# First sublayer in a written order: adaLN weights in blocks of 256 features, two feature blocks modulated at a time

## Chip, cores and metric

One core of a Trainium2 chip runs the whole program once. The metric is the device time of that execution in microseconds (us); of several runs the median is taken.

## What is computed

Two transformer blocks with adaLN modulation over 256 tokens of `x` and 256 tokens of `ctx` (1024 features, float32), then a third hybrid layer and a final norm. The change touches the start of the first half-FFN of block 0:

```python
def adaln(cond, w, b):
    m = jax.nn.silu(cond) @ w + b
    return m.reshape(m.shape[:-1] + (N_MOD, D_MODEL))
def modulated_norm(h, g, m, k):
    return rmsnorm(h, g) * (1.0 + m[..., k + 1, :]) + m[..., k, :]
def swiglu(h, w_in, w_out):
    gate, up = jnp.split(h @ w_in, 2, axis=-1)
    return (jax.nn.silu(gate) * up) @ w_out
```

`h` is both the 256 rows of `x` and the 256 rows of `ctx`, each with its own condition vector. Before the first FFN product can be made, shift `m[0]` and scale `m[1]` (1024 features each, out of `ada_w`) have to be there.

## The kernel before

All work is in float32. A product is made of three matmuls (`mm3`, L142 to L144) of operands that are split into a high part (ACT copy, L132) and a low part (DVE subtraction, L133). The kernel is written in the Tile framework: pools give out buffers, and the framework's scheduler decides in which order the instructions stand on each engine, from the written order and its own model of time. Each engine then works through its own list strictly in that order.

Pools that matter: `rawp`, 5 buffers of 512 KB for loaded weights (`wdma`, L166); `wsp`, 8 buffers for split weights; the arena `ar`, 37 units of 512 KB; `psp`, 8 banks of PSUM.

`FirstFfn.start` (from L788) loads the four 128-row tiles of `x` and `ctx` (L797), scales each row by its root mean square (`stats`, steps to L533) and then goes through eight blocks `b` of 128 features:

- `dma_mod(b)`: two loads of 512 KB from `ada_w` (shift and scale), rows of 128 features, thus 512 B in one piece.
- `mod_products(b)`: 16 matmuls (L820) of the two condition vectors with these weights, then a copy by ACT (L823); `mod_columns(b)`: one small matmul (L828), and two DVE steps to `mods` and `amod` (L831, L832).
- `turn_in(b)`: four transposes (L838) of the scaled rows; `modulate(b)`: two ACT steps (L845), then the DVE cast to the high part (L848) and subtraction for the low part (L849) of `xT`.
- `products(b, q)`: for gate (`q` 0) and up (`q` 1) weights, two column blocks of three matmuls each over 512 tokens (L142 to L144).
- `dma_w(x)` and `split_w(x)`: the two halves (512 rows each) of the first 256 columns of gate and up weights.

After `start`, `setup_late` loads the bias of block 1 and three norm vectors by ACT's queue (L251, L243) and transposes them (L253). Then `body` makes the next pair of columns: `next_pair` loads two blocks for gate and two for up, splits them and goes on. PE's first matmul of that next pair is the mark used below for the end of the stage.

Far later in the program, `DiffAttention.setup` has a function `consts`; among its steps are a load of 128 single values, `subln`, by SP's queue (L945), and one DVE step that scales them (L946). They depend on nothing of the first sublayer.

Of the kernel before, what the change touches and what calls it, by code (L numbers as in the profile page):

```python
# [9 lines left out]
AF = mybir.ActivationFunctionType  # L10
ALU = mybir.AluOpType
AX = mybir.AxisListType

P = 128
D = 1024
KB = D // P
S = 256
# [73 lines left out]
class Kern:  # L91
# [48 lines left out]
    def mm3(self, out, lhi, llo, rhi, rlo, start, stop):  # L140
        mm = self.nc.tensor.matmul
        mm(out, lhi, rhi, start=start, stop=False)  # L142
        mm(out, lhi, rlo, start=False, stop=False)  # L143
        mm(out, llo, rhi, start=False, stop=stop)  # L144
# [60 lines left out]
    def setup(self):  # L205
# [29 lines left out]
        iv = self.ident.rearrange("p (h q r) -> p h q r", h=2, q=2)  # L235
        nc.vector.tensor_tensor(self.sel, iv[:, 0, :, 0:2], iv[:, 1, :, 0:2], ALU.add)

    def setup_late(self):
        nc, a, cp = self.nc, self.a, self.cp
        self.adab.append(self.cols(a["ada_b"][1].rearrange("(k p) -> k p", p=P), 72, "adab1"))  # L240
        n2 = self.scr([24, P])
        for i, nme in enumerate(("norm_ffn1_2", "norm_mix_2", "norm_ffn2_2")):
            nc.scalar.dma_start(n2[8 * i:8 * i + 8, :], a[nme].rearrange("b (k p) -> (b k) p", p=P))  # L243
        self.n2 = self.cols(None, 24, "n2c", rows=n2)

    def cols(self, src, n, name, rows=None):

# [537 lines left out]
class FirstFfn(ModFfn):  # L785


    def start(self):  # L788
        nc, k, a = self.nc, self.k, self.a
        self.begun = self.T  # L790
        self.xT = k.asplit(KB, self.T)
        self.xn = [None] * 4
        self.p = [[k.ps() for _ in range(2)] for _ in range(2)]
        self.w = [[None, None], [None, None]]
        self.h = [k.unit([P, D]) for _ in range(4)]
        for t in range(4):
            nc.sync.dma_start(self.h[t], (a["x"] if t < 2 else a["ctx"])[0, (t % 2) * P:(t % 2 + 1) * P, :])  # L797

        mod = []
        w = [None, None]  # L800

        def dma_mod(b):
            mod.append([
                k.wdma(a["ada_w"][0, :, q * D + b * P:q * D + (b + 1) * P].rearrange("(k p) c -> p k c", p=P),
                       [P, KB, P]) for q in range(2)])

        def dma_w(x):
            w[x] = [k.wdma(src[512 * x:512 * x + 512, c0:c0 + 256].rearrange("(k p) c -> p k c", p=P), [P, 4, 256])
                    for src, c0 in (self.wg, self.wu)]

        def split_w(x):
            for q in range(2):
                self.w[q][x] = k.wsplit(w[x][q])

        def mod_products(b):
            pm = k.ps()
            for kk in range(KB):
                for q in range(2):
                    g = 32 * (2 * (kk % 2) + q)
                    nc.tensor.matmul(pm[g:g + 32, 0:P], k.sc[:, kk, :], mod[b][q][:, kk, :],  # L820
                                     start=kk < 2, stop=kk >= KB - 2)
            ms = k.scr([P, P])
            nc.scalar.activation(ms, pm[:, 0:P], AF.Copy)  # L823
            return pm, ms

        def mod_columns(b, pm, ms):
            pc = pm[:, 256:260].rearrange("p (q s) -> p q s", q=2)
            nc.tensor.matmul(pc, ms, k.sel, start=True, stop=True)  # L828
            mv = k.mods[0].rearrange("p (m k) s -> p m k s", k=KB)[:, 0:2, b, :]
            bv = k.adab[0].rearrange("p (m k) -> p m k", k=KB)[:, 0:2, b:b + 1]  # L830
            nc.vector.tensor_tensor(mv, pc, bv.to_broadcast([P, 2, 2]), ALU.add)  # L831
            nc.vector.scalar_tensor_tensor(k.amod[0][:, 0, :, b], k.mods[0][:, KB + b, :], 1.0,  # L832
                                           k.ng[:, b:b + 1].to_broadcast([P, 2]), ALU.add, ALU.mult)

        def turn_in(b):
            pt = k.ps()
            for t in range(4):
                nc.tensor.transpose(pt[:, t * P:(t + 1) * P], self.xn[t][:, b * P:(b + 1) * P], k.ident)  # L838
            return pt

        def modulate(b, pt):
            f = k.scr([P, self.T])
            for s in range(2):
                sl = slice(s * S, (s + 1) * S)
                nc.scalar.activation(f[:, sl], pt[:, sl], AF.Identity,  # L845
                                     scale=self.scale(s)[:, b:b + 1], bias=self.bias(s)[:, b:b + 1])
            hi, lo = self.xT.at(0, b), self.xT.at(1, b)
            nc.vector.tensor_copy(hi, f)  # L848
            nc.vector.tensor_tensor(lo, f, hi.bitcast(F32), ALU.subtract)  # L849

        def products(b, q):
            for c in range(2):
                hi, lo = self.w[q][b // 4]
                cc = slice(c * P, (c + 1) * P)
                k.mm3(self.p[q][c], hi[:, b % 4, cc], lo[:, b % 4, cc], self.xT.at(0, b), self.xT.at(1, b),
                      b == 0, b == KB - 1)

        dma_mod(0)
        dma_w(0)
        for b in range(1, 4):  # L860
            dma_mod(b)
        o = Order()
        for t in range(4):
            steps, took = self.stats(t)
            o.steps(1.46 * t, steps)
        o.issue()
        pt = None
        for b in range(KB + 1):
            if b < KB:
                pm, ms = mod_products(b)  # L870
                nt = turn_in(b)
            if b == 0:
                split_w(0)
            if b:
                products(b - 1, 0)
            if b < KB:
                mod_columns(b, pm, ms)
                modulate(b, nt)
            if b == 2:
                dma_w(1)  # L880
            if b == 4:
                split_w(1)
            if 2 <= b < 6:
                dma_mod(b + 2)
            if b:
                products(b - 1, 1)


class PlainFfn(Ffn, Phase):
# [835 lines left out]
```

## Time and profile before

| what | us |
|---|---|
| median of 3 runs (2332.54 to 2335.16) | 2334.33 |
| the profiled execution, its own time | 2337.68 |
| its span, first to last instruction | 2335.8 |
| first matmul of the next pair (end of the stage) | 59.76 |

Over the span PE is busy 97%, DVE 65%, ACT 46%, POOL 4%. In a timeline each row gives start, duration, engine, line, operation, output and input tiles, and in brackets the idle time ahead of it with what ended it. In a table of windows each row gives, for a stretch, the busy time of each engine with its number of instructions, the granted clock of TensorE, the mean busy share of the 16 DMA engines and the rate of the loads in GB/s.

### The profile page before, as it was taken

How to read it: one execution, taken by the hardware profiler on the slowest of the kernel's cores; microseconds unless marked ns; L12 is line 12 of the kernel's file. 1: busy time of each engine (PE TensorE's matmuls, PEld its weight loads, DVE VectorE, ACT ScalarE, POOL GpSimd, SP SyncE). 2: the span in 40 equal slices, each digit the busy share in tenths (PEclk: the TensorE clock that was granted, in tenths of full speed). 3: DMA queues.
4: the chain of work that ended last, by engine and by line, in shares of the span. 5: the costliest groups of instructions: out<-in, count | busy, mean ns of one | idle time of the engine just before them, and what ended most of it. 6: DMA issues, size and time to landing. Idle time of an engine off the chain costs nothing.

```text
span 2335.8 us, 31186 instructions
## 1 busy us (share of the span) xinstructions
PE 2269.2 (97%) x11835; PEld 1910.5 (82%) x11835; DVE 1523.0 (65%) x2478; ACT 1063.1 (46%) x1975; POOL 84.4 (4%) x130
## 2 busy tenths in 40 slices
PE   7999999998899999999999999999999999999998
PEld 5888888877688788888888887788889887898887
DVE  4876474678767753746866626676666757887664
ACT  4322223566653222134323225666556647765553
POOL 0000000111110000000000001100000002000000
PEclk9999999999999999999999999999999999999999
DMA  9665374321225543652665442145665675545664
GB/s 283 206 190 180 108 235 135 100 64 46 82 73 162 180 145 105 214 168 73 199 186 170 163 148 71 63 152 177 195 198 173 188 243 145 149 122 190 179 183 143
DMA packets 270943, 361.31 MB, mean 155 GB/s; under 512 B 11472, under 2 KB 222280, under 8 KB 270792
## 3 DMA queue, kind: packets, MB, share of 16 engines
q1 hardware_dynamic: 270464, 359.17, 49.6%
q8 instruction: 93, 1.52, 0.3%
q14 instruction: 58, 0.48, 0.1%
q10 hardware_dynamic: 328, 0.14, 0.0%
HBM read 355.02 MB, written 4.24 MB: 154 GB/s over the span
## 4 chain that ended last, share of the span: by engine, by line
PE 60%; DVE 5%; ACT 2%; POOL 1%; issue 1%; DMA 1%; POOLq 0%; DVEq 0%; ACTq 0%
PE ps L142 14%; PE ps L143 14%; PE ps L144 14%; PE ps L151 9%; PE ps L153 5%; PE ps L154 1%; DVE wl L133 1%; DVE u L133 1%; ACT junk L371 1%; DVE u L409 1%; POOL sm L377 0%; DVE s_l L556 0%; ACT wh L132 0%; PE ps L545 0%; PE ps L288 0%
## 5 line engine op out<-in xcount | busy, mean ns | idle before, releaser
L133 DVE TENSOR_TENSOR wl<-raw,wh 128x1024 fp32r<-128x1024 f32 x458 | 550.6, 1211 | 369.6 <-ACT wh L132 347.0
L132 ACT ACTIVATE wh<-raw 128x1024 fp32r<-128x1024 f32 x458 | 475.1, 1047 | 527.1 <-PE ps L143 443.7
L142 PE MATMUL ps<-s_h,wh 128*128 128x512 f32 (+1 forms) x1312 | 491.5, 376 | 6.9 <-ACT u L1063 5.0
L143 PE MATMUL ps<-s_l,wh 128*128 128x512 f32 (+1 forms) x1312 | 489.8, 373 | 0.6
L144 PE MATMUL ps<-s_h,wl 128*128 128x512 f32 (+1 forms) x1312 | 488.5, 372 | 0.0
L275 DVE SCALAR_TENSOR_TENSOR u<-raw,sc,u 128x1024 f32<-128x1024 f32 x224 | 276.9, 1279 | 81.1 <-DMA raw<-in_ada_w_dram 81.0
L142 PE MATMUL ps<-wh,s_h 128*128 128x512 f32 x784 | 308.0, 393 | 0.0
L143 PE MATMUL ps<-wl,s_h 128*128 128x512 f32 x784 | 306.1, 390 | 0.0
L144 PE MATMUL ps<-wh,s_l 128*128 128x512 f32 x784 | 305.7, 390 | 0.0
L142 PEld LDWEIGHTS ps<-s_h,wh 128*128 128x128 f32 x1312 | 247.6, 189 | 56.8 <-ACT u L1063 6.2
L143 PEld LDWEIGHTS ps<-s_l,wh 128*128 128x128 f32 x1312 | 247.4, 189 | 44.5 <-DVE s_l L556 2.3
L144 PEld LDWEIGHTS ps<-s_h,wl 128*128 128x128 f32 x1312 | 247.5, 189 | 42.5
L151 PE MATMUL ps<-s_p,wh 128*128 128x512 f32 x1008 | 258.1, 395 | 1.4 <-DVE scr L160 1.4
L151 PEld LDWEIGHTS ps<-s_p,wh 128*128 128x128 f32 x1008 | 188.1, 189 | 37.6 <-DVE scr L160 1.3
L132 ACT ACTIVATE s_h<-scr 128x256 fp32r<-128x256 f32 (+1 forms) x144 | 73.3, 510 | 247.4 <-DVE scr L724 230.5
L144 PEld LDWEIGHTS ps<-wh,s_l 128*128 128x128 f32 x784 | 147.6, 188 | 31.0
L142 PEld LDWEIGHTS ps<-wh,s_h 128*128 128x128 f32 x784 | 147.8, 189 | 30.4 <-DVE scr L1115 0.2
L143 PEld LDWEIGHTS ps<-wl,s_h 128*128 128x128 f32 x784 | 147.7, 188 | 29.9
L153 PEld LDWEIGHTS ps<-s_p,wl 128*128 128x128 f32 x1152 | 157.9, 191 | 11.5
L153 PE MATMUL ps<-s_p,wl 128*128 128x256 f32 x1152 | 161.3, 283 | 0.0
L143 PE MATMUL ps<-u,s_h 128*128 128x512 f32 x264 | 103.9, 393 | 1.3 <-DVE u L133 1.3
L142 PE MATMUL ps<-u,s_h 128*128 128x512 f32 x264 | 104.2, 395 | 0.0
(209 smaller groups left out, 2735.0 us busy)
## 6 DMA issues: line engine op xcount, KB each, us to landing
raw<-in_ffn_w_in_dram SPq DMA_DIRECT2D x176, 512.0 KB, 4.3
raw<-in_ada_w_dram SPq DMA_DIRECT2D x144, 512.0 KB, 4.5
raw<-in_ffn_w_out_dram SPq DMA_DIRECT2D x88, 512.0 KB, 4.3
raw<-in_ffn_gate_dram SPq DMA_DIRECT2D x44, 512.0 KB, 4.8
raw<-in_ffn_up_dram SPq DMA_DIRECT2D x44, 512.0 KB, 4.7
raw<-in_ffn_down_dram SPq DMA_DIRECT2D x44, 512.0 KB, 4.4
raw<-in_w_in_dram SPq DMA_DIRECT2D x44, 512.0 KB, 4.3
raw<-in_da_w_in_dram SPq DMA_DIRECT2D x24, 512.0 KB, 3.8
```

The costliest lines, as they stand in the source:

```text
L132: self.nc.scalar.activation(hi, src, AF.Copy)
L133: self.nc.vector.tensor_tensor(lo, src, hi.bitcast(F32), ALU.subtract)
L142: mm(out, lhi, rhi, start=start, stop=False)
L143: mm(out, lhi, rlo, start=False, stop=False)
L144: mm(out, llo, rhi, start=False, stop=stop)
L151: mm(out, w(b)[0], x.both(b), start=b == 0, stop=False)
L153: mm(out[:, 0:S], w(b)[1], x.at(0, b), start=False, stop=False)
L154: mm(out, w(n - 1)[0], x.both(n - 1), start=False, stop=True)
L275: nc.vector.scalar_tensor_tensor(acc[s][h], raw, x, acc[s][h], ALU.mult, ALU.add)
L371: self.nc.scalar.activation(self.junk, src, AF.Square, scale=1.0 / 32, accum_out=ss)
L409: nc.vector.scalar_tensor_tensor(h[:, sl], st.yg[k], st.r, h[:, sl], ALU.mult, ALU.add)
```

## The change

- `ada_w` comes in pieces for two feature blocks: per pair `bp` four loads of 512 KB (rows of 256 features, 1 KB in one piece; 512 of the 1024 input rows each), straight into arena units and no longer into `rawp`.
- One pair's `mod_products` has 16 matmuls over 256 columns; `mod_columns` makes both blocks. So two blocks are modulated at a time.
- The units of the scaled rows are given out first (`o.issue()` stands before `dma_mod(1)`).
- Order by hand: the whole stage stands inside `with k.tc.manual_schedule()`; loads are issued up front, products of block `b` stand beside the preparation of later blocks.
- `setup_late`'s loads move to SP's queue at the end of the stage's loads (`load_late`), into an arena unit.

```diff
+    def load_late(self):
+        nc, a = self.nc, self.a
+        rows = self.unit([P, 2, P])
+        self.late_rows = rows[0:72, 0, :], rows[0:24, 1, :]
+        nc.sync.dma_start(self.late_rows[0], a["ada_b"][1].rearrange("(k p) -> k p", p=P))
+        for i, nme in enumerate(("norm_ffn1_2", "norm_mix_2", "norm_ffn2_2")):
+            nc.sync.dma_start(rows[8 * i:8 * i + 8, 1, :], a[nme].rearrange("b (k p) -> (b k) p", p=P))
...
-        def dma_mod(b):
-            mod.append([
-                k.wdma(a["ada_w"][0, :, q * D + b * P:q * D + (b + 1) * P].rearrange("(k p) c -> p k c", p=P),
-                       [P, KB, P]) for q in range(2)])
+        def dma_mod(bp):
+
+            mod.append([[k.unit([P, 4, S]) for _ in range(2)] for _ in range(2)])
+            for x in range(2):
+                for q in range(2):
+                    c0 = q * D + bp * S
+                    nc.sync.dma_start(mod[bp][q][x], a["ada_w"][0, 512 * x:512 * x + 512, c0:c0 + S]
+                                      .rearrange("(k p) c -> p k c", p=P))
...
-        dma_mod(0)
-        dma_w(0)
-        for b in range(1, 4):
-            dma_mod(b)
         o = Order()
         for t in range(4):
             steps, took = self.stats(t)
             o.steps(1.46 * t, steps)
-        o.issue()
-        pt = None
-        for b in range(KB + 1):
...
+        with k.tc.manual_schedule():
+
+            dma_w(0, 0)
+            dma_mod(0)
+            dma_w(1, 0)
+            o.issue()
+            dma_mod(1)
+            dma_mod(2)
+            for q in range(2):
+                dma_w(q, 1)
+            dma_mod(3)
+            k.load_late()
+            NP = KB // 2
+            turned = {0: turn_in(0)}
+            split_w(0, 0)
+            pm = mod_products(0)
+            turned[1] = turn_in(1)
+            mod_columns(0, *pm)
+            modulate(0, turned.pop(0))
+            split_w(1, 0)
+            modulate(1, turned.pop(1))
+            for bp in range(NP):
+                b = 2 * bp
+                last = bp == NP - 1
+                products(b, 0)
+                if bp == 0:
+                    products(b, 1)
+                if not last:
+                    pm = mod_products(bp + 1)
+                    turned[b + 2] = turn_in(b + 2)
+                if bp:
+                    products(b, 1)
+                if not last:
+                    mod_columns(bp + 1, *pm)
+                    modulate(b + 2, turned.pop(b + 2))
+                products(b + 1, 0)
+                if not last:
+                    turned[b + 3] = turn_in(b + 3)
+                    modulate(b + 3, turned.pop(b + 3))
+                if bp == 1:
+                    for q in range(2):
+                        split_w(q, 1)
+                products(b + 1, 1)
```

Where this puts instructions is seen in the order of the built programs. Names in brackets are the semaphores that an instruction waits for: `DMAHW0` to `DMAHW7` are eight counters that the loads are given in turn, so that a load first waits for the one that had its counter before.

DVE, before, near the end of the stage (`s_h_121` is the high part of blocks 6 and 7, `wl` the low parts of the next pair's weights):

```order
L133 TENSOR_TENSOR wl_608<-raw_603,wh_607 128x1024 [waits DMAHW5_49,Activation_49]
L848 CAST s_h_121<-scr_516 128x512 [waits Activation_49]
L849 TENSOR_TENSOR s_l_122<-scr_516,s_h_121 128x512 [waits DVE_49]
L133 TENSOR_TENSOR wl_612<-raw_605,wh_611 128x1024 [waits DMAHW6_49,Activation_49]
L946 TENSOR_SCALAR subln<-subln 128x1 [waits DMAHW0_49]
L831 TENSOR_TENSOR mods_103<-ps_527,adab_95 128x2x2 [waits PE_49]
L832 SCALAR_TENSOR_TENSOR amod_105<-mods_103,ng 128x2 [waits DVE_49]
```

DVE, changed, near its beginning (`s_h_115` is the high part of blocks 0 and 1, `s_h_117` that of blocks 2 and 3):

```order
L133 TENSOR_TENSOR wl_267<-raw_147,wh_266 128x1024 [waits DMAHW6_49,Activation_49]
L860 CAST s_h_115<-scr_270 128x512 [waits Activation_49]
L861 TENSOR_TENSOR s_l_116<-scr_270,s_h_115 128x512 [waits DVE_49]
L843 TENSOR_TENSOR mods_103<-ps_287,adab_95 128x2x2 [waits PE_49,Activation_49]
L844 SCALAR_TENSOR_TENSOR amod_105<-mods_103,ng 128x2 [waits DVE_49]
L843 TENSOR_TENSOR mods_103<-ps_287,adab_95 128x2x2
L844 SCALAR_TENSOR_TENSOR amod_105<-mods_103,ng 128x2 [waits DVE_49]
L976 TENSOR_SCALAR subln<-subln 128x1 [waits DMAHW4_49]
L860 CAST s_h_117<-scr_317 128x512 [waits Activation_49]
L861 TENSOR_TENSOR s_l_118<-scr_317,s_h_117 128x512 [waits DVE_49]
```

The step on `subln` stood behind the splits of the next pair's first weights and ahead of block 7; it now stands ahead of the high part of block 2.

SP's queue, before, near the end of the stage (`raw_603` and `raw_605` are the next pair's gate weights, `raw_627` and `raw_629` its up weights):

```order
L166 DMA raw_475<-in_ada_w_dram 128x8x128 [waits DMAHW7_49,PE_49]
L166 DMA raw_603<-in_ffn_w_in_dram 128x4x256 [waits DMAHW0_49,PE_49]
L166 DMA raw_605<-in_ffn_w_in_dram 128x4x256 [waits DMAHW1_49,PE_49]
L166 DMA raw_627<-in_ffn_w_in_dram 128x4x256 [waits DMAHW2_49,PE_49]
L945 DMA subln<-in_da_subln_dram 128x1
L166 DMA raw_629<-in_ffn_w_in_dram 128x4x256 [waits DMAHW5_49,DVE_49]
```

SP's queue, changed, from the last pair's four pieces on (`u_209` to `u_212`):

```order
L813 DMA u_209<-in_ada_w_dram 128x4x256 [waits DMAHW1_49]
L813 DMA u_211<-in_ada_w_dram 128x4x256 [waits DMAHW2_49]
L813 DMA u_210<-in_ada_w_dram 128x4x256 [waits DMAHW3_49]
L813 DMA u_212<-in_ada_w_dram 128x4x256 [waits DMAHW4_49]
L242 DMA u_217<-in_ada_b_dram 72x128 [waits DMAHW5_49]
...
L166 DMA raw_529<-in_ffn_w_in_dram 128x4x256 [waits DMAHW1_49]
L166 DMA raw_531<-in_ffn_w_in_dram 128x4x256 [waits DMAHW2_49,DVE_49]
L166 DMA raw_553<-in_ffn_w_in_dram 128x4x256 [waits DMAHW3_49,DVE_49]
L975 DMA subln<-in_da_subln_dram 128x1 [waits DMAHW4_49]
```

The load of `subln` stands in the same company as before, behind the next pair's blocks. Before, it waited for no counter; now it has the one that `u_212`, the last piece of `ada_w`, had before it.

ACT, changed, behind the two modulations of blocks 4 and 5 (`raw_205` and `raw_207` are the second halves of the first gate and up weights, `raw_529` and `raw_531` the next pair's gate weights):

```order
L857 ACTIVATE scr_402<-ps_397,mods_103,amod_105 128x256 [waits DVE_49,PE_49,Activation_49]
L857 ACTIVATE scr_402<-ps_397,mods_103,amod_105 128x256
L132 ACTIVATE wh_407<-raw_205 128x1024 [waits DMAHW7_49]
L132 ACTIVATE wh_411<-raw_207 128x1024 [waits DMAHW0_49]
L132 ACTIVATE wh_533<-raw_529 128x1024 [waits DMAHW1_49]
L132 ACTIVATE wh_537<-raw_531 128x1024 [waits DMAHW2_49,PE_49]
L832 ACTIVATE scr_444<-ps_427 128x256 [waits PE_49,Activation_49]
```

Before, the same splits stood ahead of the modulation of block 3 (lines L132 between L823 and L845):

```order
L132 ACTIVATE wh_417<-raw_317 128x1024 [waits DMAHW3_49]
L823 ACTIVATE scr_348<-ps_331 128x128 [waits PE_49,Activation_49]
L132 ACTIVATE wh_421<-raw_319 128x1024 [waits DMAHW4_49]
L845 ACTIVATE scr_364<-ps_350,mods_103,amod_105 128x256 [waits DVE_49,PE_49,Activation_49]
L845 ACTIVATE scr_364<-ps_350,mods_103,amod_105 128x256
```

They now follow the modulation of block 5, and block 4 is the first that uses them. From about the 270th row of PE on, the order on all engines is the same as before.

## Rows read from the trace of the kernel before

**Rows 1.** Windows of 10 us: busy time of each engine, granted clock, DMA share, GB/s.
```profile
20.00:30.00 10.00, 10.00 (x96) 7.40 (x94) 2.05 (x7) 2.45 (x6) 0.00 (x0) 1.00 1.12 298
50.00:60.00 10.00, 7.87 (x38) 5.43 (x34) 5.73 (x12) 5.12 (x9) 0.00 (x0) 1.00 0.66 230
60.00:70.00 10.00, 10.00 (x45) 8.26 (x45) 7.60 (x11) 3.24 (x4) 0.00 (x0) 1.00 0.57 190
```
**Rows 2.** Timeline of PE: first modulation, first product, one steady block, the stage's end.
```profile
14.51 1.93 PE L820 MATMUL ps<-raw,sc 128*32 128x128 f32 x30
...
19.93 1.63 PE L142 MATMUL ps<-s_h,wh 128*128 128x512 f32 x3
...
25.46 1.08 PE L820 MATMUL ps<-raw,sc 128*32 128x128 f32 x32
26.47 0.66 PE L838 MATMUL ps<-ident,u 128*128 128x128 f32 x4
26.89 0.47 PE L142 MATMUL ps<-s_h,wh 128*128 128x512 f32 x1
...
28.36 0.28 PE L828 MATMUL ps<-sel,scr 128*128 128x4 f32 x2
28.49 0.47 PE L142 MATMUL ps<-s_h,wh 128*128 128x512 f32 x1
...
30.06 1.08 PE L820 MATMUL ps<-raw,sc 128*32 128x128 f32 x32
...
59.12 0.25 PE L253 MATMUL ps<-ident,scr 72*128 72x72 f32 x1 [0.82 <-DMA scr<-in_ada_b_dram]
59.76 0.50 PE L142 MATMUL ps<-s_h,wh 128*128 128x512 f32 x1
```
**Rows 3.** Windows, for the rate of the loads (last column, GB/s).
```profile
0.00:9.00 9.00, 0.73 (x3) 0.46 (x3) 1.50 (x11) 3.99 (x9) 0.76 (x5) 1.00 0.73 256
9.00:12.00 3.00, 0.00 (x0) 0.00 (x0) 1.67 (x7) 2.87 (x9) 1.11 (x2) 1.00 1.18 303
53.00:57.00 4.00, 3.42 (x16) 2.52 (x15) 1.50 (x5) 1.02 (x2) 0.00 (x0) 1.00 1.04 388
7.00:8.00 1.00, 0.00 (x0) 0.00 (x0) 0.11 (x1) 0.94 (x5) 0.00 (x0) 1.00 1.01 410
```
**Rows 4.** Timeline of SP's queue: issue of a small load at the start, and of `subln`.
```profile
0.74 0.38 SPq L208 DMA_DIRECT2D ident<-in_k_ident_dram  x1
...
41.47 5.03 SPq L166 DMA_DIRECT2D raw<-in_ffn_w_in_dram  x3
46.54 0.50 SPq L945 DMA_DIRECT2D subln<-in_da_subln_dram  x1
```
**Rows 5.** Timeline of DVE: the step that waits for `ident`, and the stage's end.
```profile
2.93 0.16 DVE L236 TENSOR_TENSOR sel<-ident 128x4 f32<-128x4 f32 x1 [1.56 <-DMA ident<-in_k_ident_dram]
...
50.70 0.42 DVE L848 CAST s_h<-scr 128x512 fp32r<-128x512 f32 x1
51.16 0.69 DVE L849 TENSOR_TENSOR s_l<-scr,s_h 128x512 fp32r<-128x512 f32 x1
51.77 1.22 DVE L133 TENSOR_TENSOR wl<-raw,wh 128x1024 fp32r<-128x1024 f32 x1
53.22 0.15 DVE L946 TENSOR_SCALAR subln<-subln 128x1 f32<-128x1 f32 x1 [0.23 <-DMA subln<-in_da_subln_dram]
```
**Rows 6.** Timeline of ACT: one block's modulation and one split.
```profile
29.13 1.02 ACT L845 ACTIVATE scr<-ps,mods,amod 128x256 f32<-128x256 f32 x2 [2.22 <-DVE amod L832]
30.18 1.06 ACT L132 ACTIVATE wh<-raw 128x1024 fp32r<-128x1024 f32 x1
```
**Rows 7.** A long idle of PE far behind the stage, and the granted clock around it.
```profile
1976.13 0.69 PE L1431 MATMUL ps<-ident,u 128*128 128x128 f32 x2 [4.04 <-DVE u L1421]
...
1976.00:1981.00 5.00, 4.87 (x16) 4.20 (x17) 3.78 (x13) 2.22 (x8) 0.00 (x0) 0.50 0.36 105
1981.00:1982.00 1.00, 1.00 (x7) 0.92 (x6) 0.00 (x0) 0.05 (x1) 0.00 (x0) 0.62 0.00 0
```

More of the change, by code (lines that the diff above doesn't have):

```diff
@@ L236, in setup @@
         nc.vector.tensor_tensor(self.sel, iv[:, 0, :, 0:2], iv[:, 1, :, 0:2], ALU.add)
-    def setup_late(self):
[L239 to L244, printed above, removed]
+    def load_late(self):
[5 more added lines that the diff above has]
+            nc.sync.dma_start(rows[8 * i:8 * i + 8, 1, :], a[nme].rearrange("b (k p) -> (b k) p", p=P))
+    def setup_late(self):
+        self.adab.append(self.cols(None, 72, "adab1", rows=self.late_rows[0]))
+        self.n2 = self.cols(None, 24, "n2c", rows=self.late_rows[1])
+        del self.late_rows
     def cols(self, src, n, name, rows=None):
@@ L799, in start, with dma_w, split_w, mod_products @@
         mod = []
-        w = [None, None]
-        def dma_mod(b):
-            mod.append([
-                k.wdma(a["ada_w"][0, :, q * D + b * P:q * D + (b + 1) * P].rearrange("(k p) c -> p k c", p=P),
-                       [P, KB, P]) for q in range(2)])
[L807 to L815, printed above, removed]
+        w = {}
+        def dma_mod(bp):
[5 more added lines that the diff above has]
+                                      .rearrange("(k p) c -> p k c", p=P))
+        def dma_w(q, x):
+            src, c0 = (self.wg, self.wu)[q]
+            w[q, x] = k.wdma(src[512 * x:512 * x + 512, c0:c0 + 256].rearrange("(k p) c -> p k c", p=P), [P, 4, 256])
+        def split_w(q, x):
+            self.w[q][x] = k.wsplit(w[q, x])
+        def mod_products(bp):
             pm = k.ps()
@@ L819, in mod_products, with mod_columns @@
                     g = 32 * (2 * (kk % 2) + q)
-                    nc.tensor.matmul(pm[g:g + 32, 0:P], k.sc[:, kk, :], mod[b][q][:, kk, :],
+                    nc.tensor.matmul(pm[g:g + 32, 0:S], k.sc[:, kk, :], mod[bp][q][kk // 4][:, kk % 4, :],
                                      start=kk < 2, stop=kk >= KB - 2)
-            ms = k.scr([P, P])
-            nc.scalar.activation(ms, pm[:, 0:P], AF.Copy)
+            mod[bp] = None
+            ms = k.scr([P, S])
+            nc.scalar.activation(ms, pm[:, 0:S], AF.Copy)
             return pm, ms
[L826 to L833, printed above, removed]
+        def mod_columns(bp, pm, ms):
+            pc = pm[:, S:S + 8].rearrange("p (b q s) -> p b q s", b=2, q=2)
+            for x in range(2):
+                nc.tensor.matmul(pc[:, x], ms[:, x * P:(x + 1) * P], k.sel, start=True, stop=True)
+            for x in range(2):
+                b = 2 * bp + x
+                mv = k.mods[0].rearrange("p (m k) s -> p m k s", k=KB)[:, 0:2, b, :]
+                bv = k.adab[0].rearrange("p (m k) -> p m k", k=KB)[:, 0:2, b:b + 1]
+                nc.vector.tensor_tensor(mv, pc[:, x], bv.to_broadcast([P, 2, 2]), ALU.add)
+                nc.vector.scalar_tensor_tensor(k.amod[0][:, 0, :, b], k.mods[0][:, KB + b, :], 1.0,
+                                               k.ng[:, b:b + 1].to_broadcast([P, 2]), ALU.add, ALU.mult)
         def turn_in(b):
@@ L865, in start @@
             o.steps(1.46 * t, steps)
-        o.issue()
-        pt = None
-        for b in range(KB + 1):
[L869 to L886, printed above, removed]
+        with k.tc.manual_schedule():
[40 more added lines that the diff above has]
+                products(b + 1, 1)
 class PlainFfn(Ffn, Phase):
```

## The prediction

> **What bounds the kernel now.** I read the table of windows first. From 20 us on PE has no gap for thirty microseconds; between 50 and 60 us it is busy 7.87 of 10, and from 60 us on it is full again [rows 1]. Loads run at 298 GB/s beside it with the DMA engines marked as saturated (share 1.12) [rows 1]. So two resources are close to their limit in the stage, PE and the loads, and what the change can win lies in the gaps at its two ends.
>
> The timeline of PE gives the rhythm [rows 2]. A steady block starts with its modulation at 25.46 us and the next with its own at 30.06: 4.60 us. Of that the modulation's matmuls take 1.01 (25.46 to 26.47), the transposes 0.42 (to 26.89), the column matmul 0.13 (28.36 to 28.49), and the twelve products the rest, 3.04, so 1.52 for one half block. The first product starts at 19.93, the next pair's first matmul, which I take as the end of the stage, at 59.76; just ahead of it PE waits 0.82 us for a late load [rows 2]. From there on the order of all engines is unchanged and PE is full, so the difference at this mark passes on to the end.
>
> **What the change does, part by part.**
>
> *The step on `subln` in DVE's list decides.* In the order of the changed program DVE meets `subln` right behind the second pair of `mods`/`amod`, and the cast of block 2 is queued behind it. DVE takes its steps in that order. PE needs this cast for `products(2, 0)`, and everything PE has behind that, the modulation of blocks 4 and 5 included, stands behind it in PE's list. Before, the same step stood near the end of the stage and cost 0.23 us of DVE's time [rows 5].
>
> When does `subln` land? SP issues its load only when the counter it takes over has been released, that is when `u_212`, the last piece of `ada_w` for the stage, has landed. Up to there the stage has loaded 2.10 MB of `x` and `ctx`, 20 pieces of 512 KB (16 of `ada_w`, 4 of gate and up weights; 10.49 MB) and 0.16 MB of constants, 12.75 MB. By 9.0 us 256 GB/s have brought 2.30 MB [rows 3], and that part is unchanged in kind. For the other 10.45 MB the rate is open: 303 GB/s is what a stretch with much 512 B traffic shows, 388 one with rows of 1 KB and 4 KB, 410 one with 4 KB rows alone [rows 3]. The new pieces all have rows of 1 KB, so 388 is nearest: 26.9 us, landing at **35.9 us** (34.5 at 410, 43.5 at 303).
>
> Then the load itself. Before, SP issued it at 46.54 behind three blocks of weights issued from 41.47 on [rows 4], and DVE could go on at 53.22 [rows 5]: 6.7 us. Now it again stands behind three blocks of the next pair. The other end is a small load with nothing ahead of it, `ident`: issued at 0.74 [rows 4], used at 2.93 [rows 5], 2.2 us. I take 6.7, since the company is the same: DVE is released at **42.6 us** (38.1 by the other end). With 0.15 for the step, 0.42 for the cast [rows 5] and about 0.1 for the signal, PE goes on at 43.2.
>
> *What is left for PE from there*, all on the path: blocks 2 to 7 have 12 half blocks of 1.52, 18.2 us; two modulations (pairs 2 and 3); transposes of blocks 4 to 7, 4 times 0.42, 1.7; four column matmuls of 0.13, 0.5 [rows 2]. A modulation now has the same 16 matmuls over 256 columns in place of 128: between 1.01, if a matmul's cost is fixed, and 2.02, if it goes by columns; I take 2.02, as the columns are what streams, so 4.0. Together 24.5.
>
> *The clock.* While DVE waits, PE idles: blocks 0 and 1 are done by about 31 to 35 us, so for 8 us or more. Far behind, PE waits 4.04 us and then runs at a granted clock of 0.50, the 1.2 GHz level, from 1976.13 until about a quarter before 1982 [rows 7]: 5.6 us at half rate, 2.8 us lost. I add 2.8; the ends are 0 and, if it stays low twice as long, 5.6.
>
> *The splits of the second halves.* ACT now has them behind the modulation of block 5, and block 4's products are the first to need them. From the end of block 5's transposes: 1.02 us for its modulation and 1.06 for the split [rows 6], so the high part is there after 2.1, while PE has only one half block of 1.52 ahead: 0.6 us of wait. DVE has the cast, 0.42, the low part, 0.69, then the weights' low part, 1.22 [rows 5], ready after 3.4 to 3.5, which PE's third matmul wants at about 2.6: 0.8 to 0.9. Together **1.5 us** (0 if the half clock keeps PE behind).
>
> *Edits with no cost or gain here.* The first load order, the wider first modulation and the new order of blocks 0 and 1 all lie ahead of PE's wait and are covered by it; without that cover they are the first rival. The late loads now land long before they are wanted, which takes the 0.82 us away [rows 2]; the two transposes keep about 0.4. Raw buffers are no longer held by `ada_w`, so the next pair's weights are split inside the stage; the second pair of splits was so before.
>
> *Sum.* 43.2 + 24.5 + 2.8 + 1.5 + 0.4 = 72.4 us against 59.76: **12.6 us more**. The profiled execution takes 2337.68 us in all around a span of 2335.8, 3.35 above the median of the runs; it would become 2350.3, and the median of 2334.33 becomes **2346.9 us**, 0.54% more. About 0.2%, 4.7 us, can be told from no change.
>
> **A rule against this sum.** The row of mixed 512 B traffic gives 303 GB/s, the row with longer pieces 388 [rows 3]; I read that as a gain of the longer pieces. The Trainium skill ("DMA: Bandwidth & Descriptors", Specifications) says that transfers reach line rate from 512 B on, which would leave the loads as slow as they are. The two rows speak against it here. What would follow is worked out next, from the slower row.
>
> **The rivals.**
>
> - *The loads do not get faster.* At 303 GB/s the last piece lands at 43.5 us and the three blocks ahead of `subln` pass in 6.7 times 388/303, 8.6: DVE is released at 52.1, and the end is 9.5 later, 2356.4 us. For it: most of what the stage loads is still `ada_w`, and other limits than the row length may hold there. Against it: 388 and 410 GB/s in the same execution [rows 3]. Chance 0.08.
> - *`subln` lands soon after its issue*, 2.2 us as `ident`, because little is left of the blocks ahead: 38.1 in place of 42.6, so 2342.4 us. For it: these blocks are issued up to 4 us earlier than `subln`. Against it: before, they were too [rows 4]. Chance 0.13.
> - *DVE does not wait* (not slower). It decides as soon as `subln` lands before about 28 to 31 us, when block 2 is due. Then PE's work counts from the start. The first four pieces and one weight block land at 15.6 us (4.88 MB less 2.30, at 388). The first modulation runs at the slow rate of the beginning, 30 matmul rows in 1.93 us where 32 later take 1.01 [rows 2], so 4.1 for 256 columns, half of it behind the last piece: 17.7. Before, the first product came 3.5 us behind the modulation's end (16.44 to 19.93) [rows 2]: 21.2. From there eight blocks, 24.3, and three modulations, six transposes and six column matmuls, 9.4, with 1.5 for the splits, 0.4, and some 1.5 of slow clock: 58.3 against 59.76, so 2332.9 us. Against it: the release of the counter needs 10.45 MB more, and no row shows the 500 GB/s that this would take. Chance 0.06.
>
> **How the numbers follow.** The forecast has 0.73. Its own ends: 410 GB/s takes 1.4 off, cheap modulations 2.0, no wait for splits 1.5, no slow clock 2.8, not all together; the slow clock for twice as long adds 2.8, a rate halfway to 303 some 4.5. That is 2342 to 2352. With the second rival the range of **2340.5 to 2353** leaves out the other two and a little of the tails. Faster by over 0.2%: 0.03, from the third rival's better part. Within 0.2%: 0.05, the rest of it and a wait of which almost nothing is left. Slower: 0.92.
>
> **What would show it.** In the profile after, DVE's row on `subln` with several microseconds of idle time ahead of it, put down to its load, starting near 42.6; PE idle by 8 us or more ahead of the first product of block 2; a granted clock of 0.50 behind it, if the records have it; loads near 390 GB/s until 36 us; small waits of PE ahead of block 4; the next pair's first matmul near 72. The forecast is wrong if DVE's row on `subln` has no idle time, or if PE's stage ends before 64.

## The result, and the profile after

| what | before | changed |
|---|---|---|
| median, us | 2334.39 (4 runs, 2332.54 to 2335.16) | 2346.86 (4 runs, 2346.12 to 2347.06) |
| profiled execution, its own time, us | 2337.68 | 2346.92 |
| its span, us | 2335.8 | 2345.2 |
| mean granted clock of TensorE | 0.993 | 0.991 |
| first matmul of the next pair, us | 59.76 | 73.92 |

The changed kernel is 0.53% slower: ratio 1.0053, 95% interval 1.0041 to 1.0065. At the mark that the prediction uses, the next pair's first matmul, it is 14.16 us late.

Lines have moved: L828 is now the modulation, L838 the column matmul, L850 the transposes, L860 and L861 the high and low part of `xT`, L975 and L976 the load and the scale of `subln`.

The table of windows answers to [rows 1] and [rows 3] (busy time per engine, granted clock, DMA share, GB/s):

```profile
20.00:30.00 10.00, 8.10 (x54) 5.23 (x55) 3.78 (x9) 3.26 (x6) 0.00 (x0) 0.83 1.09 348
30.00:40.00 10.00, 3.03 (x16) 2.15 (x14) 0.40 (x3) 2.04 (x4) 0.00 (x0) 0.85 1.09 348
60.00:70.00 10.00, 10.00 (x75) 7.51 (x74) 5.76 (x11) 3.45 (x7) 0.00 (x0) 1.00 0.64 212
...
10.00:43.00 33.00, 17.83 (x111) 10.24 (x111) 7.78 (x21) 8.30 (x19) 1.10 (x2) 0.86 1.09 348
```

PE is busy 3.03 of 10 us from 30 to 40, ACT 2.04 and DVE 0.40. Only the loads go on, at 348 GB/s. The queue of SP (answering to [rows 4]) and then DVE (to [rows 5]) show for what:

```profile
36.43 3.45 SPq L166 DMA_DIRECT2D raw<-in_ffn_w_in_dram  x3
40.98 0.35 SPq L975 DMA_DIRECT2D subln<-in_da_subln_dram  x1
```

```profile
30.28 0.16 DVE L844 SCALAR_TENSOR_TENSOR amod<-mods,ng 128x2 f32<-128x2 f32 x1
45.69 0.15 DVE L976 TENSOR_SCALAR subln<-subln 128x1 f32<-128x1 f32 x1 [15.25 <-DMA subln<-in_da_subln_dram]
45.76 0.42 DVE L860 CAST s_h<-scr 128x512 fp32r<-128x512 f32 x1
```

SP is done with the three weight blocks at 39.88 (36.43 and 3.45). Only the last 1.1 us up to 40.98 is its wait for the counter of `u_212`; up to then the load of `subln` stood in SP's queue behind all loads of the stage. No run took the counter away alone. DVE stands still for 15.25 us ahead of a step of 0.15 us whose result is first wanted at 524 us, and the cast of block 2 starts 0.07 us after it. PE, answering to [rows 2]:

```profile
21.67 0.49 PE L142 MATMUL ps<-s_h,wh 128*128 128x512 f32 x1 [2.02 <-DVE s_h L860]
...
26.64 1.94 PE L828 MATMUL ps<-u,sc 128*32 128x256 f32 x32
...
46.23 0.80 PE L142 MATMUL ps<-s_h,wh 128*128 128x512 f32 x1 [13.20 <-DVE s_h L860]
...
58.23 0.49 PE L142 MATMUL ps<-s_h,wh 128*128 128x512 f32 x1 [0.71 <-ACT wh L132]
...
59.61 0.50 PE L144 MATMUL ps<-s_h,wl 128*128 128x512 f32 x1 [0.64 <-DVE wl L133]
...
60.73 1.93 PE L828 MATMUL ps<-u,sc 128*32 128x256 f32 x32
62.60 0.66 PE L850 MATMUL ps<-ident,u 128*128 128x128 f32 x4
...
73.60 0.39 PE L258 MATMUL ps<-ident,u 72*128 72x72 f32 x2
73.92 0.50 PE L142 MATMUL ps<-s_h,wh 128*128 128x512 f32 x1
```

PE waits 13.20 us for that cast. Ahead of block 4 come the two waits for the splits, 0.71 and 0.64. The first product of block 2 takes 0.80 where the others take 0.50, and the windows around it say why (same columns):

```profile
37.00:38.00 1.00, 0.00 (x0) 0.00 (x0) 0.00 (x0) 0.00 (x0) 0.00 (x0) 0.50 1.09 348
46.00:47.00 1.00, 0.77 (x2) 0.33 (x2) 0.97 (x3) 0.00 (x0) 0.00 (x0) 0.50 0.00 0
50.00:51.00 1.00, 1.00 (x20) 0.46 (x15) 0.00 (x0) 0.00 (x0) 0.00 (x0) 0.70 0.00 0
51.00:52.00 1.00, 1.00 (x22) 0.41 (x11) 0.00 (x0) 0.00 (x0) 0.00 (x0) 1.00 0.00 0
```

The granted clock fell to 0.50 (1.2 GHz) while PE stood still and stayed there for the first 4.5 us or so of its work. The 0.83 from 20 to 30 us in the first table is an earlier stretch of low clock, behind the first product; it lies ahead of PE's wait and is covered by it.

**From 14.16 us to 9.4.** At the mark the changed kernel is 14.16 us late, and at L545 (now L550) still 14.2 (399.9 against 414.1), but at that line's last pass only 8.9 (2146.9 against 2155.8), and the spans differ by 9.4. Past 560 us both kernels have stretches at a low clock, and the execution of before has more of them. Its windows, and those of the changed kernel at the same work some 10 us later:

```profile
1500.00:1505.00 5.00, 3.13 (x18) 2.16 (x15) 4.55 (x10) 4.56 (x13) 0.00 (x0) 0.89 0.03 11
1505.00:1510.00 5.00, 5.00 (x29) 4.38 (x28) 3.06 (x8) 2.64 (x6) 0.00 (x0) 0.77 0.00 0
2140.00:2145.00 5.00, 5.00 (x27) 4.34 (x27) 2.41 (x8) 2.31 (x8) 0.08 (x1) 0.78 0.26 85
```

```profile
1510.00:1515.00 5.00, 3.57 (x17) 1.33 (x15) 4.55 (x13) 4.76 (x16) 1.01 (x1) 1.00 0.39 134
1515.00:1520.00 5.00, 3.77 (x29) 3.33 (x30) 4.63 (x10) 4.26 (x10) 0.00 (x0) 1.00 0.00 0
2150.00:2155.00 5.00, 4.68 (x31) 3.96 (x29) 3.23 (x10) 3.59 (x9) 0.55 (x1) 1.00 0.41 133
```

Summed over 5 us windows up to the end of PE's work (2330 us before, 2340 us changed), length times (1 minus granted clock) is 15.5 us in the execution of before, all of it past 560 us, and 10.2 us past 560 us in that of the changed kernel. The difference, 5.3 us, is what is missing at the last pass of that line (14.2 less 8.9). This is a reckoning from the clock column; no run tried it. Another 0.5 us, from 8.9 to 9.4, comes behind that pass and is not in these sums. The medians differ by 12.5, since the profiled execution of before is 3.3 above its own median.

### The profile page after: what moved, and what is told of

It reads as the page before. It is cut to its first block, busy times and chain, and to the rows that moved or that the text cites. A ratio compares the mean times of both kernels' runs of the same rounds, so it can differ in the third digit from the quotient of the medians.

```text
span 2345.2 us, 30906 instructions
## 1 busy us (share of the span) xinstructions
PE 2266.1 (97%) x11707; PEld 1903.8 (81%) x11707; DVE 1522.5 (65%) x2478; ACT 1061.7 (45%) x1971; POOL 83.3 (4%) x130
## 4 chain that ended last, share of the span: by engine, by line
PE 58%; DVE 6%; ACT 3%; POOL 1%; issue 1%; DMA 1%; POOLq 0%; DVEq 0%; ACTq 0%
PE ps L142 14%; PE ps L143 14%; PE ps L144 14%; PE ps L151 9%; PE ps L153 5%; PE ps L154 1%; DVE u L133 1%; DVE wl L133 1%; ACT junk L376 1%; DVE u L414 1%; ACT wh L132 0%; ACT u L132 0%; POOL sm L382 0%; DVE s_l L561 0%; PE ps L550 0%
## 5 line engine op out<-in xcount | busy, mean ns | idle before, releaser
L132 ACT ACTIVATE wh<-raw 128x1024 fp32r<-128x1024 f32 x458 | 474.9, 1047 | 527.8 <-PE ps L143 448.9
L132 ACT ACTIVATE s_h<-scr 128x256 fp32r<-128x256 f32 (+1 forms) x144 | 73.2, 510 | 235.3 <-DVE scr L729 218.1
```

Source lines behind the costliest of these rows:

```text
L132: self.nc.scalar.activation(hi, src, AF.Copy)
```

## The experiments

The theory: the place of `subln`'s step in DVE's list, together with the late issue of its load, makes all of the loss. The rivals: the written order is slow of itself; the wider loads or the slow clock make the loss; DVE's place does not matter and only the time of the landing does.

**e1: the step on another engine.** Nothing else moves.

```diff
-            nc.vector.tensor_scalar(self.sub, self.sub, 1.0 - lam_init, None, ALU.mult)
+            nc.gpsimd.tensor_scalar(self.sub, self.sub, 1.0 - lam_init, None, ALU.mult)
```

> One word differs from the changed kernel: the step that scales subln is made by POOL and no longer stands in DVE's list; all loads and all other lists stay as they are. Theory (the wait of DVE on subln sets the time): the cast of block 2 starts as soon as ACT has its input, near 31.3 us, PE goes on at about 32.9 instead of 46.2, and the clock does not fall, which gives back another 2.2; the next pair starts near 58.3 instead of 73.9 and the time is 2331 us (2329 to 2334), a little under the kernel before. Rival (block 2 would wait for something else as well, its weights, its modulation or the loads in general): PE still idles by 5 us or more ahead of block 2 and the time stays above 2340 us.

Measured: 2330.97 us (11 runs, 2328.75 to 2335.28), ratio to before 0.998, 0.9971 to 0.9989. POOL's timeline, then PE's:

```profile
46.04 1.02 POOL L976 TENSOR_SCALAR subln<-subln 128x1 f32<-128x1 f32 x1 [33.13 <-DMA subln<-in_da_subln_dram]
```

```profile
58.75 0.39 PE L258 MATMUL ps<-ident,u 72*128 72x72 f32 x2
59.07 0.50 PE L142 MATMUL ps<-s_h,wh 128*128 128x512 f32 x1
```

The wait is still there, 33.13 us long, on an engine that has nothing else to do there. The load lands as late as before (46.04), the next pair comes at 59.07 in place of 73.92, and 15.9 us of time go. One wait made the whole loss, and what costs is what stands behind it.

**e2: the load at the start, the step still on DVE.** The load is the first of ACT's queue, and DVE takes the step at 3.0 us.

```diff
+        self.sub = cp.tile([P, 1], F32, name="subln")
+        nc.scalar.dma_start(self.sub, a["da_subln"].rearrange("b d -> d b"))
...
-            self.sub = k.cp.tile([P, 1], F32, name="subln")
-            nc.sync.dma_start(self.sub, a["da_subln"].rearrange("b d -> d b"))
+            self.sub = k.sub
```

> The load of subln is issued at the very start by ACT's queue; its scaling stays with DVE. Theory: no wait in the stage, as with the step on POOL: next pair near 58.3, 2331 us, within 1.5 us of the run with POOL. Rival: the load at the start delays something there (the bias rows behind it on ACT's queue, or DVE's first steps, which would stand behind the scaling), and the stage ends 1 to 3 us later than with POOL.

Measured: 2332.38 us (11 runs, 2329.23 to 2336.18), ratio 0.9988, 0.998 to 0.9997. The row of the step among those of its tile (durations in ns, then the first and the last start), and PE's timeline:

```profile
L977 DVE TENSOR_SCALAR subln<-subln x1: 154/154/154, 3.0 to 3.0; 128x1 f32<-128x1 f32 x1
```

```profile
59.84 0.50 PE L142 MATMUL ps<-s_h,wh 128*128 128x512 f32 x1
```

The loss is gone here too. But the edit moves two things: the load is issued at 0.7 us, and the step now stands at the beginning of DVE's list and no longer behind the second pair of `mods`/`amod`. So e2 does not show what the old place in the list would cost with the data already there; no run has that.

**e3: pieces of 512 B.** Every load of `ada_w` is made as two loads of 128 features, all else as in the changed kernel.

```diff
-                    nc.sync.dma_start(mod[bp][q][x], a["ada_w"][0, 512 * x:512 * x + 512, c0:c0 + S]
-                                      .rearrange("(k p) c -> p k c", p=P))
+                    for y in range(2):
+                        nc.sync.dma_start(mod[bp][q][x][:, :, y * P:(y + 1) * P],
+                                          a["ada_w"][0, 512 * x:512 * x + 512, c0 + y * P:c0 + (y + 1) * P]
+                                          .rearrange("(k p) c -> p k c", p=P))
```

> Each piece of ada_w is loaded in two loads of 128 features (512 B in one piece) into the same unit; the rest is unchanged, the wait on subln included. Theory (longer pieces load faster): 8.4 MB come at some 295 GB/s and not at 348, so the last piece, subln and with it DVE's release come about 4 to 5 us later, near 50 us, and the time is 2351 us (2349 to 2354). Rival (512 B is as good as 1 KB): the rate stays near 348 GB/s, DVE is released near 45.7 and the time stays at 2347 us.

Measured: 2353.26 us (4 runs, 2352.5 to 2353.98), ratio 1.0075, 1.0061 to 1.0089. A window of the loads, and PE's timeline:

```profile
9.00:33.00 24.00, 17.20 (x112) 9.76 (x111) 8.44 (x24) 9.49 (x21) 1.65 (x3) 1.00 1.20 301
```

```profile
51.91 0.79 PE L142 MATMUL ps<-s_h,wh 128*128 128x512 f32 x1 [18.69 <-DVE s_h L862]
...
79.45 0.50 PE L142 MATMUL ps<-s_h,wh 128*128 128x512 f32 x1
```

The loads run at 301 GB/s in place of 348 and `subln` lands 5.7 us later, at 51.4. From PE's resumption to the next pair it takes 27.54 us, against 27.69 in the changed kernel (46.23 to 73.92): the end follows the landing one to one. The time rose by 6.4, within what was expected. The edit also halves each load to 256 KB. The 512 KB loads with pieces of 512 B in the kernel before ran at 303 GB/s [rows 3], so the slower rate is there without that.

**e4: PE kept busy during the wait.** 52 useless matmuls are added ahead of block 2; the rest is as in the changed kernel.

```diff
+                if bp == 1:
+                    warm = k.ps()
+                    for _ in range(52):
+                        nc.tensor.matmul(warm, self.w[0][0][0][:, 0, 0:P], self.xT.at(0, 0), start=True, stop=True)
```

> The changed kernel with 52 matmuls of no use (128x512 into a spare bank) put on PE ahead of the first product of block 2; they fill some 12 of the 13 us in which PE waits. Theory (the fall of the clock costs about 2.2 us of the stage): the granted clock stays at 1.00 up to block 2's products, the next pair starts near 71.7 instead of 73.9 and the time is 2344.6 us. Rival (the slow clock is hidden behind DVE's and ACT's work): 2346.9 us, no difference.

Measured: 2348.18 us (5 runs, 2344.09 to 2349.55), ratio 1.0049, 1.0036 to 1.0062. Window and PE's timeline:

```profile
30.00:60.00 30.00, 28.02 (x162) 20.94 (x162) 8.21 (x20) 8.63 (x14) 0.00 (x0) 1.00 0.51 161
```

```profile
34.44 11.95 PE L901 MATMUL ps<-s_h,wh 128*128 128x512 f32 x52
46.77 0.49 PE L142 MATMUL ps<-s_h,wh 128*128 128x512 f32 x1 [0.39 <-DVE s_h L860]
...
72.85 0.50 PE L142 MATMUL ps<-s_h,wh 128*128 128x512 f32 x1
```

The clock stayed at 1.00, and block 2 to the next pair took 26.08 us in place of 27.69. So the slow clock costs 1.6 us of the 14.16. In the total nothing of it can be seen: the runs of e4 lie on both sides of the changed kernel's, and neither expected time is confirmed.

**e5 and e6: what else stands in PE's way.** Both have the step on POOL. e5 takes the splits of the second halves ahead of block 2's products; e6 also loads the first gate weights behind the first modulation's pieces.

```diff
                 last = bp == NP - 1
+                if bp == 1:
+                    for q in range(2):
+                        split_w(q, 1)
...
-                if bp == 1:
-                    for q in range(2):
-                        split_w(q, 1)
```

> The scale of subln on POOL, as in e1, and the second-half splits moved ahead of the first products of block 2. In e1 PE still stood still 0.72 us for the high part and 0.65 us for the low part of these weights ahead of block 4. Theory (these two waits are on PE's path, and ACT and DVE have room for the splits earlier): both waits are gone, the next pair's first matmul comes at 57.7 us in place of 59.07, and the time is 2329.6 us, 1.4 under e1. Rival (the splits then hold up the cast of block 2 or 3, each being 1.1 us of ACT and 1.2 us of DVE, so that a wait of the same size stands ahead of block 2): next pair at 59 us or later, time 2331.

```diff
-            dma_w(0, 0)
             dma_mod(0)
+            dma_w(0, 0)
...
-            split_w(0, 0)
             pm = mod_products(0)
+            split_w(0, 0)
```

> As e5, and the first weight block is loaded behind the four pieces of the first modulation, not ahead of them, its split written behind that modulation. Theory: the first modulation's last piece lands 512 KB sooner (1.3 to 1.5 us at 350 to 400 GB/s), the first product starts near 21.4 us in place of 22.74, and the next pair at 56.4; time 2328.3 us. Rival: the first weights are now the last thing the first product waits for (they land where the last piece landed, and their split on ACT and DVE, 1.1 and 1.2 us, follows), so the first product starts at 22.7 or later and the time is e5's, 2329.6.

Measured: e5 2327.45 us (7 runs, 2325.95 to 2333.54), ratio 0.9973, 0.9962 to 0.9985; e6 2331.28 us (11 runs, 2328.98 to 2335.98), ratio 0.9987, 0.9979 to 0.9996. PE in e5, and then in e10, which is e1 run once more (below):

```profile
22.01 0.49 PE L142 MATMUL ps<-s_h,wh 128*128 128x512 f32 x1 [2.02 <-DVE s_h L860]
...
55.68 0.50 PE L142 MATMUL ps<-s_h,wh 128*128 128x512 f32 x1
```

```profile
21.45 0.49 PE L142 MATMUL ps<-s_h,wh 128*128 128x512 f32 x1 [2.02 <-DVE s_h L860]
...
40.84 0.50 PE L142 MATMUL ps<-s_h,wh 128*128 128x512 f32 x1 [0.73 <-ACT wh L132]
...
42.22 0.50 PE L144 MATMUL ps<-s_h,wl 128*128 128x512 f32 x1 [0.64 <-DVE wl L133]
...
56.51 0.50 PE L142 MATMUL ps<-s_h,wh 128*128 128x512 f32 x1
```

Neither execution has a low clock in the stage. From first product to next pair e10 takes 35.06 us and e5 33.67: the 1.39 between them are the two waits, 1.37, which e5 does not have. e6 did not do what was expected. Its DVE:

```profile
19.23 1.23 DVE L133 TENSOR_TENSOR wl<-raw,wh 128x1024 fp32r<-128x1024 f32 x1 [5.22 <-ACT wh L132]
20.38 0.16 DVE L843 TENSOR_TENSOR mods<-ps,adab 128x4 f32<-128x4 f32 x1
```

The split of the first weights now stands between the modulation's matmuls and its `mods` on DVE. `mods` starts at 20.38 (20.08 in e5), and the first product at 22.30; the next pair comes at 56.83, with a granted clock of 0.83 from 20 to 30 us. The column matmul ahead of it ends at 19.45 in e6 and at 19.99 in e5. So the earlier pieces gave 0.5 us, and the split took 0.9. Against e5 the next pair comes 1.15 us later and the median is 3.8 us higher; e5's execution has no low clock, and how much of the rest is due to that stays open.

**e7: the same edit on the kernel before**, where the step had waited 0.23 us [rows 5]. The order on PE is the one of before.

> The kernel before with the scale of subln on POOL; all other instructions keep their order. Theory (there the step waited 0.23 us on DVE, and PE did not wait for DVE at that place): no change, 2334.4 us, within 0.1% of the kernel before. Rival (the step costs something on DVE wherever it stands, and e1's gain of 15.9 us on the changed kernel is partly a general one): faster than the kernel before by 1 us or more.

Measured: 2332.5 us (11 runs, 2330.53 to 2337.03), ratio 0.999, 0.9981 to 0.9999. The kernel before, measured beside it, has 2334.48, so e7 is 2.0 us faster; its next pair comes at 59.47 in place of 59.76. Both expectations are met, within 0.1% of 2334.4 and faster by over 1 us, so the run does not decide between them. The edit is worth 15.9 us on one kernel and some 2 on the other, by the interval at most 4.4. It also says how small a ratio should be believed: e1's 0.2% against before, with next pairs 0.7 us apart, is hardly more.

**e8: e3 and e1 together**, the pieces of 512 B with the step on POOL.

> The changed kernel with each piece of adaLN weights loaded in two loads of 128 features (512 B in one piece), as in e3, and the scale of subln on POOL, as in e1. Theory (the 5.2 us that e3 lost against the changed kernel's stage, and the 6.4 us in its time, came only through the later landing of subln; with the step off DVE the loads are hidden but for the first modulation): the last piece lands near 44 us, PE wants the last pair's at 45.9; PE waits only ahead of the first modulation, 0.4 to 1 us more than in e1; next pair at 59.5 to 60, time 2331.5 to 2332. Rival (the slower loads hold up later modulations or the weights behind them): PE waits for adaLN weights ahead of the third or fourth modulation, next pair at 62 or later, time over 2334.

Measured: 2334.53 us (10 runs, 2331.23 to 2335.53), ratio 0.9994, 0.9984 to 1.0003. Window and PE's timeline:

```profile
10.00:43.00 33.00, 27.16 (x179) 16.86 (x179) 12.23 (x33) 11.22 (x25) 1.12 (x3) 0.95 1.20 300
```

```profile
18.82 1.06 PE L830 MATMUL ps<-u,sc 128*32 128x256 f32 x14 [0.71 <-DMA u<-in_ada_w_dram]
...
46.47 1.93 PE L830 MATMUL ps<-u,sc 128*32 128x256 f32 x32
...
60.31 0.50 PE L142 MATMUL ps<-s_h,wh 128*128 128x512 f32 x1
```

The wait for adaLN weights is ahead of the first modulation alone, as the theory had it; the last modulation (46.47) does not wait. At the next pair the small pieces cost 1.24 us against e1 (60.31 to 59.07; both executions have a granted clock of 0.83 from 20 to 30 us), a little over the 1 us allowed. The time is 2.5 us over the upper end of what was expected, and past the rival's 2334, without the rival's wait. With `subln` in the way the same pieces cost 5.5 us at the next pair (79.45 to 73.92). So at this mark most of what the longer pieces bring in the changed kernel, they bring to a wait that need not be there. The times show less of that: 6.4 us between e3 and the changed kernel, 3.6 between e8 and e1. Where the 2.3 us come from that the mark does not show stays open.

**e9: the late loads on ACT's queue.** The step on `subln` then stands one block earlier in DVE's list, and its load behind one block of weights.

```diff
-        nc.sync.dma_start(self.late_rows[0], a["ada_b"][1].rearrange("(k p) -> k p", p=P))
+        nc.scalar.dma_start(self.late_rows[0], a["ada_b"][1].rearrange("(k p) -> k p", p=P))
...
-            nc.sync.dma_start(rows[8 * i:8 * i + 8, 1, :], a[nme].rearrange("b (k p) -> (b k) p", p=P))
+            nc.scalar.dma_start(rows[8 * i:8 * i + 8, 1, :], a[nme].rearrange("b (k p) -> (b k) p", p=P))
```

> The changed kernel with the late loads (bias and three norm vectors of block 1) on ACT's queue in place of SP's. The scheduler then puts subln's step of DVE one block earlier, ahead of the cast of blocks 0 and 1, and its load behind one block of the next pair's weights, on the counter of the last but two piece of adaLN weights. Theory (what counts is which cast stands behind the step, times when subln lands): it is issued near 38 us and lands near 42.6, DVE and then PE start block 0 at 43.2 and have eight blocks left, the 36.3 us that e1 took from its first product to the next pair: 79.5 us, time 2352.5 us. Rival (only the landing counts, and it comes 3 us earlier): next pair at 71, time 2344.

Measured: 2351.45 us (4 runs, 2350.4 to 2353.74), ratio 1.0072, 1.0058 to 1.0086; next pair at 79.49. ACT's and DVE's timelines:

```profile
34.98 1.06 ACT L132 ACTIVATE wh<-raw 128x1024 fp32r<-128x1024 f32 x1 [22.63 <-DMA u<-in_ada_w_dram]
```

```profile
42.57 0.15 DVE L976 TENSOR_SCALAR subln<-subln 128x1 f32<-128x1 f32 x1 [4.48 <-DMA subln<-in_da_subln_dram]
42.64 0.42 DVE L860 CAST s_h<-scr 128x512 fp32r<-128x512 f32 x1
```

PE's timeline:

```profile
36.36 1.01 PE L838 MATMUL ps<-sel,scr 128*128 128x4 f32 x4 [16.01 <-ACT scr L832]
43.11 0.80 PE L142 MATMUL ps<-s_h,wh 128*128 128x512 f32 x1 [5.74 <-DVE s_h L860]
...
79.49 0.50 PE L142 MATMUL ps<-s_h,wh 128*128 128x512 f32 x1
```

`subln` lands 3.1 us earlier than in the changed kernel, and the next pair comes 5.6 us later, because eight blocks stand behind it in place of six: the rival, by which the landing alone counts, falls. One thing was not foreseen: ACT stood still for 22.63 us, because the late loads on its queue wait for counters that earlier loads hold; they are issued at 30.14, 31.64, 33.14 and 34.66. It is the same trap on another engine; it ended earlier, and DVE's wait for `subln` came last. By itself ACT's wait would have made most of the lateness too: it held the column matmul up by 16.01 us, and without `subln` the first cast would have come near 38.9 in place of 42.64 (an estimate: the last `amod` starts at 37.93, and in the changed kernel the cast follows it by 0.98). So e9 shows that the blocks behind the step count, and not that the wait for `subln` alone costs the 20.4 us between e9 and e1 at this mark.

**e10 and e11: e1 and e5 once more**, side by side.

> e1 once more, the same kernel, beside e5's, to see what of their difference repeats on one chip. Theory (the granted clock of 0.50 from 22.7 us on comes with the idle of PE around the first modulation and belongs to this order): dip again, next pair at 59.1, time 2331. Rival (the dip is a matter of the execution): no dip, next pair near 57.

> e5 once more, the same kernel. Theory (splits earlier take 1.37 us of waits away, and the rest of the 3.4 us between e1 and e5 at the next pair is the dip): if the dip is a matter of the execution, next pair at 55.7 without it or 57.7 with it, time 1 to 4 us under e1's of the same call. Rival (e5's 2327.45 was a matter of the chip): time within 1 us of e1's.

Measured: e10 2331.76 us (11 runs, 2328.69 to 2335.12), ratio 0.9989, 0.998 to 0.9998; e11 2328.5 us (8 runs, 2326.34 to 2333.15), ratio 0.9977, 0.9967 to 0.9987. The next pair comes at 56.51 in e10 and at 56.14 in e11. The low clock near 23 us does not belong to the order of the instructions: e1 had it and e10, the same kernel, not; e5 not and e11, the same kernel, had it (0.83 from 20 to 30 us). The two of each pair ran on different chips, so the chip and the execution cannot be told apart. With the low clock 57.7 was expected of e11, so it cost less there than in e1: from first product to next pair 0.6 us more than in e5, where e1 took 1.3 more than e10. The median of e5's order is 3.3 us under that of e1's where both ran on one chip (e11, e10) and 3.5 us on two (e5, e1). That is more than the 1.4 us of waits, but the runs overlap widely and so do the intervals of the ratios of e10 and e11, so more than the waits is not shown. In the profiled executions e5 lost 6.8 us by the clock sum used above and e10 12.0. Why an order changed in the stage should alter the clock far behind it, and whether it does, stays open. This order is the fastest seen: 0.23 to 0.27% under the kernel before, 0.8% under the changed one.

## Why the prediction was right

The forecast was 2346.9 us, and 2346.86 was measured. The mechanism is the one named: DVE's step on `subln` ahead of block 2's cast, released by the counter of the last adaLN piece. e1 shows it by taking the step off DVE, where nothing else moves, and e3 by a later landing, which the stage's end follows. But the agreement to 0.04 us is luck: terms of the sum were off in both directions.

| step | predicted, us | measured, us |
|---|---|---|
| counter released, `subln` issued | 35.9 | 40.98 |
| issue to DVE | 6.7 | 4.7 |
| DVE released, PE goes on | 42.6, 43.2 | 45.69, 46.23 |
| rest of the stage at full clock (24.5 + 1.5 + 0.4) | 26.4 | 26.08 (e4) |
| slow clock | 2.8 | 1.6 (27.69 less 26.08) |
| next pair | 72.4 | 73.92 |
| later against before at the next pair | 12.6 | 14.16 |
| profiled execution against before | 12.6 | 9.2 |

- *The rate of the loads* was the term most off: 388 GB/s was chosen as the nearest row, 348 came. That row was not one of 1 KB: of the 1.55 MB it moved, 1.05 MB came in 256 packets of 4 KB. The kernel before had a nearer one, a microsecond in which 0.34 MB came in 369 packets, all under 2 KB, and the DMA share was that of the changed kernel:

```profile
27.00:28.00 1.00, 1.00 (x7) 0.82 (x6) 0.00 (x0) 0.00 (x0) 0.00 (x0) 1.00 1.09 337
```

At 348 the 10.45 MB take 30.0 us and end at 39.0. The other 2.0 us up to the issue are not part of the sum as it was written: by 40.98 the loads had brought 13.4 MB (2.30 and 32 us at 348), 0.7 more than the 12.75 of the stage, which I read as the weight blocks queued behind sharing the rate with the last piece; no run tried that apart.

- *Issue to landing* gave 2.0 us back; 6.7 was from the stretch before [rows 4, rows 5]. In e8, behind the same blocks, it took 6.7 again, in e3 5.8; what sets it no run shows. Its rival, 2.2 us as for `ident`, was further off.
- *The first rival* (303 GB/s) was wrong about pieces of 1 KB and right about 512 B. The rule beside it, of the Trainium skill ("DMA: Bandwidth & Descriptors", Specifications), that transfers reach line rate from 512 B on, is not what these runs show: at 512 B and a share of 1.20 the loads ran at 301 GB/s in e3 and 300 in e8, at 1 KB and 1.09 at 348.
- *The rest of PE's work* was right to 0.3 us, its parts too: a modulation of 256 columns took 1.87 (60.73 to 62.60) where 2.02 was taken and 128 columns took 1.01, so it goes nearly by columns; the waits for the splits took 0.71 and 0.64, where 0.6 and 0.9 were taken.
- *The slow clock* came as expected, and cost 1.6 where 2.8 was taken from a stretch of 5.6 us; here it lasted some 4.5.
- *The third rival*, no wait of DVE, was priced at 2332.9 us with the next pair at 58.3. e1, e2 and e10, which remove the wait, gave 2330.97, 2332.38 and 2331.76, with 59.07, 59.84 and 56.51.
- *"The difference at this mark passes on to the end"* failed by 4.8 us in the profiled execution. By the reckoning above the instructions passed it on and the granted clock did not.

## What to carry to other kernels

When a stage is moved into a written order, look at what the scheduler now puts between its steps: a step of 0.15 us that belongs to a later layer cost 12.5 us, because its load stood behind all loads of the stage, the last of which had its counter, and an engine that works in order stood behind the step. Such a step is best given to an engine with nothing behind it (e1), or load and step are put at the start (e2). The price of a wait is what stands behind it in the list and when its data lands, both (e3, e9), so a faster load that shortens such a wait is worth less once the wait is gone (e8: 1.24 us in place of 5.5 at the next pair, 3.6 in place of 6.4 in the time).

## What the runs showed of the hardware

- The rate of saturated loads into the arena went with the piece: 300 to 301 GB/s at 512 B, 348 at 1 KB. The kernel before had 303 at 512 B, 388 with rows of 1 KB and 4 KB, and 410 with 4 KB alone [rows 3].
- A load of 128 single values took 4.5 us (e9) to 6.7 us (e8, issued at 45.4, used at 52.1) to land in nearly the same company.
- The same kernel got a low clock near 23 us in one execution and not in another, on another chip (e1, e10), and differed by 2.56 us at the next pair, of which 1.29 was already there at the first product.
